# A decoder trunk on one core: six weight tiles of the output projection's second column block ahead of the tiles that meet the last heads

## The chip, the cores and the metric

The kernel runs on one core of one Trainium2 chip. The metric is the device time of one execution in microseconds (us), lower is better; the median of several runs is compared. The engines are TensorE (PE in the profile; its weight loads are PEld), VectorE (DVE), ScalarE (ACT), GpSimd (POOL) and SyncE (SP), which here issues DMA transfers. Each engine takes its own instructions in a fixed order.

## The reference

One decoder layer on 256 tokens of width 2048, all in float32. What matters here is the middle: the gated DeltaNet output of 16 heads of 128, gated, plus a gated pooling branch, goes through one output projection with a residual; its result is normalised and enters the MLP.

```python
o = rmsnorm(o, gdn_norm_w[l]) * jax.nn.silu(z.reshape(bsz, seq, N_HEADS, HEAD_DIM))
y_a = o.reshape(bsz, seq, D_LIN)
...
mixed = jax.nn.sigmoid(g_a) * y_a + jax.nn.sigmoid(g_b) * y_b
x = x + jnp.einsum('bsd,de->bse', mixed, w_out[l])

h = rmsnorm(x, norm_ffn_w[l])
gate, up = jnp.split(jnp.einsum('bsd,df->bsf', h, w_up[l]), 2, axis=-1)
```

`mixed` is 256 x 2048 and `w_out` is 2048 x 2048. The sum over d for one output column needs all 16 heads.

## The kernel before, in words

**Weights.** Every weight matrix is streamed once, as tiles of 256 rows by 512 columns (512 KB), in one list `srcs` (L79 to L95) that fixes the order of loading. For each tile `begin` (L105 to L120) starts a load into `raw` (four buffers) on SP's queue, a cast into `whi` on ScalarE (L112) and the rest `raw - whi` into `wlo` on VectorE (L119). `whi` and `wlo` have three buffers each. `weights()` hands out the next tile of the list and starts those up to two tiles further on (`AHEAD = 2`). A buffer is written again when the matmuls that read it are done.

**Matmuls.** `gemm_a` (L138 to L153) makes a 256 x 512 block of a product. A weight tile covers two steps k of 128 rows; for each, and each half t of the tokens, there are three matmuls of 128x128 by 128x512: high part of the activations times `whi` (L149), low part times `whi` (L150), high part times `wlo` (L151). So a weight tile is twelve matmuls, and a block of 2048 rows is eight tiles. The block accumulates in a PSUM tile of the pool `psm`, of which there are two (L62). With `steps` and `ps` a call does only some of the tiles and goes on with a PSUM tile begun before.

**Heads.** The heads are made in four groups g of four. The small matmuls and vector work of a group are dealt out by `side()` between the big matmuls of the input projection. When a group is through, `gated` (L779) forms its gated sum `sz` (L781, L782), and `mixed` (L791) transposes `sz` on PE (`turned`, eight transposes, L194) into PSUM; ScalarE copies that to `mhi` (L794) and VectorE takes the rest to `mlo` (L795). `mhi[g]`, `mlo[g]` are the activations of rows 512g to 512g + 511 of the output projection. Its weight tiles 6 and 7 of each block, and only those, meet group 3.

**The output projection.** Four column blocks of 512. Since group 3 is finished last, L805 begins the first blocks with the tiles that do not need it: tiles 0 to 5 of block 0 and 0, 1 of block 1, in the two PSUM tiles. Then come `gated` and `mixed` of group 3, the end of the pool `mix`, the load of x into `xt` on ScalarE's queue (L813), the rest of blocks 0 and 1, and blocks 2 and 3. After each block VectorE adds its PSUM tile to `xt` (L823), which frees it, ScalarE takes sums of squares (L826), PE transposes the block (L832), and ScalarE and VectorE scale it into `fhl` (L836, L837), the input of the MLP. The MLP's first matmuls are `gemm_b` (L173, L174).

**Order.** The kernel is written as one stream of instructions. Before it is built, a planner (the tile framework, with `schedule_with_timeline_sim=True`) fixes each engine's order from its own estimate of times; an instruction that is not ready by that estimate can stand behind one that comes later in the source. On the chip nothing is reordered.

Of the kernel before, what the change touches and what calls it, by code (L numbers as in the profile page):

```python
# [17 lines left out]
KD = D // P  # L18
# [15 lines left out]
def kernel(  # L34
# [32 lines left out]
    def nm(s):  # L67
        cnt[0] += 1
        return f"{s}_{cnt[0]}"

    def pg(shape=(P, 512)):
        return psg.tile(list(shape), F32, tag="g", name=nm("psg"))


    def cols(w, base, nk):
        return [w[c * 256 : (c + 1) * 256, base : base + 512].rearrange("(k p) f -> p k f", p=P)
                for c in range(nk // 2)]

    srcs = []  # L79
# [8 lines left out]
            srcs += cols(w_in[0], base + 512 * g, KD)  # L88
    outw = [cols(w_out[0], 512 * c, KD) for c in range(4)]

    srcs += outw[0][:6] + outw[1][:2] + outw[0][6:] + outw[1][2:] + outw[2] + outw[3]
    for c in range(DFF // 512):
        srcs += cols(w_up[0], 512 * c, KD) + cols(w_up[0], DFF + 512 * c, KD)
    down = [cols(w_down[0], 512 * c, KF) for c in range(4)]
# [4 lines left out]
    def weights():  # L99

        begin(taken[0] + AHEAD + 1)
        taken[0] += 1
        return made[taken[0] - 1]
# [21 lines left out]
    def side():  # L125
        next(side_work[0], None)
# [5 lines left out]
    def pm():  # L132
        return psm.tile([P, 2, 512], F32, tag="m", name=nm("psm"))
# [4 lines left out]
    def gemm_a(lh, ll, nk, steps=None, ps=None):  # L138

        ps = pm() if ps is None else ps  # L140
        for c in range(nk // 2) if steps is None else steps:
            if c == 1:
                while later:
                    later.pop(0)()
            hi, lo = weights()
            for kk in range(2):
                k = 2 * c + kk
                for t in range(2):
                    mm(ps[:, t, :], lh(k, t), hi[:, kk, :], start=(k == 0), stop=False)  # L149
                    mm(ps[:, t, :], ll(k, t), hi[:, kk, :], start=False, stop=False)  # L150
                    mm(ps[:, t, :], lh(k, t), lo[:, kk, :], start=False, stop=(k == nk - 1))  # L151
                side()
        return ps  # L153
# [3 lines left out]
    def gemm_b(rhl, nk):  # L157

        banks[0] ^= 1
        if banks[0]:
            pair = [pm(), pm()]
            ps = [pair[f // 2][:, f % 2].rearrange("p (a s) -> p a s", a=2) for f in range(4)]
        else:
            ps = [pg([P, 2, S]) for f in range(4)]
        for c in range(nk // 2):
            hi, lo = weights()
            for f in range(4):
                fs = slice(f * P, (f + 1) * P)  # L170
                for kk in range(2):
                    k = 2 * c + kk
                    mm(ps[f], hi[:, kk, fs], rhl(k), start=(k == 0), stop=False, skip_group_check=True)  # L173
                    mm(ps[f][:, 1, :], lo[:, kk, fs], rhl(k)[:, 0, :], start=False, stop=(k == nk - 1),  # L174
                       skip_group_check=True)
        return ps
# [242 lines left out]
    for g, win in enumerate(WINDOWS):  # L419
# [3 lines left out]
        for cs in (slice(0, P + PAD), slice(P + PAD, NB)):  # L423
            b = bd[:, cs]
            n = cs.stop - cs.start
# [15 lines left out]
    mhi = []  # L441
    mlo = []
# [277 lines left out]
    for g in range(4):  # L720
        kq = mp.tile([P, 4, 2, S], F32, tag="kq", bufs=1, name=nm("kq"))
        for kind, dst in ((1, kq[:, :, 0, :]), (0, kq[:, :, 1, :])):
            ps = ps_k0 if kind == 1 and g == 0 else gemm_a(xh, xl, KD)
# [15 lines left out]
        ps = gemm_a(xh, xl, KD)  # L739
# [26 lines left out]
        ps = gemm_a(lambda k, t: phi[:, k, t * P : (t + 1) * P], lambda k, t: plo[:, k, t * P : (t + 1) * P], 4)  # L766
# [4 lines left out]
        ps = gemm_a(xh, xl, KD)  # L771
# [7 lines left out]
        def gated(sz=sz, res=res, yb=yb):  # L779
            drain()  # L780
            nc.vector.tensor_tensor(sz, res[0].rearrange("p t h d -> p t (h d)"), sz, op=ALU.mult)  # L781
            nc.vector.tensor_tensor(sz, sz, yb, op=ALU.add)  # L782
# [17 lines left out]
    def at(tiles):  # L800
        return lambda k, t: tiles[k // 4][:, k % 4, t * P : (t + 1) * P]

    early = [gemm_a(at(mhi), at(mlo), KD, range(n)) for n in (6, 2)]  # L805
    gated()
    mixed()
    mix.__exit__(None, None, None)
# [7 lines left out]
    ssq4 = cpool.tile([P, 2, 4], F32, tag="ssq4", name="ssq4b")  # L816
    for c in range(4):
        if c < 2:
            ps = gemm_a(at(mhi), at(mlo), KD, range((6, 2)[c], 8), early[c])
        else:  # L820
            ps = gemm_a(at(mhi), at(mlo), KD)
        xs = xt[:, :, c * 512 : (c + 1) * 512]
        nc.vector.tensor_tensor(xs, xs, ps, op=ALU.add)  # L823
        for t in range(2):
            jk = cpool.tile([P, 512], F32, tag="sqj", name=nm("sqj"))
            nc.scalar.activation(jk, xs[:, t, :], AF.Square, accum_out=ssq4[:, t, c : c + 1])  # L826
        for k2 in range(2):
            pt = pg([P, 2, S])
            for kk in range(2):
                k = 4 * c + 2 * k2 + kk  # L830
                for t in range(2):
                    nc.tensor.transpose(pt[:, kk, t * P : (t + 1) * P], xt[:, t, k * P : (k + 1) * P], ident)  # L832
            for kk in range(2):
                k = 4 * c + 2 * k2 + kk
                nw = vec[:, V_FFN + k : V_FFN + k + 1]
                nc.scalar.activation(fhi[:, k, :], pt[:, kk, :], AF.Copy, scale=nw)  # L836
                nc.vector.scalar_tensor_tensor(flo[:, k, :], pt[:, kk, :], nw, fhi[:, k, :].bitcast(F32),  # L837
                                               op0=ALU.mult, op1=ALU.subtract)
# [9 lines left out]
    for c in range(DFF // 512):  # L848
        ps = gemm_b(lambda k: fhl[:, k], KD)
# [12 lines left out]
        ps = gemm_b(lambda k: fhl[:, k], KD)  # L862
# [15 lines left out]
    for c in range(2):  # L878
        ps = pm()
# [72 lines left out]
```

## Time and profile before

| | |
|---|---|
| median of 3 runs | 1586.81 us (1585.77 to 1587.41) |
| the profiled execution | 1584.99 us, its span 1582.9 us, mean granted clock 0.997 |
| bytes read from HBM | 297.56 MB, 191 GB/s over the span |
| w_out tiles | 32 loads of 512 KB, median 3.8 us to landing |
| casts L112, subtractions L119 | 530 of 1053 ns, 528 of 1224 ns |

A row of a timeline gives the start in us, the duration in us, the engine, the line, the operation, what it writes and reads, how many were merged (x), and in brackets how long the engine stood idle before it and what released it. A row of a table by windows gives the window, its length, and the busy time of each engine in it with the number of instructions (x), then the granted clock, the DMA engines' busy share and GB/s. Matmuls overlap one another in the records, so the pace is read from their starts.

### The profile page before, as it was taken

The numbers are of one execution on the slowest core, as the hardware profiler recorded it, in microseconds if no ns is written. First come the engines' busy times: TensorE is split into PE (matmuls) and PEld (weight loads), VectorE is DVE, ScalarE is ACT, GpSimd is POOL, SyncE is SP. The second block draws the span as 40 slices with busy tenths as digits, with TensorE's granted clock in tenths as the row PEclk, the third lists the DMA queues.
The fourth block names the chain that finished last, engine by engine and source line by source line (L and its number), as shares of the span: only waits on it lengthen the run. The fifth ranks groups of instructions, "written<-read, shape, count | busy, mean of one in ns | idle before, by whom it ended". The sixth has DMA issues, their size and how long they took to land.

```text
span 1582.9 us, 21262 instructions
## 1 busy us (share of the span) xinstructions
PE 1561.9 (99%) x8052; PEld 1311.6 (83%) x8052; DVE 1067.9 (67%) x1619; ACT 746.3 (47%) x953; POOL 44.5 (3%) x69
## 2 busy tenths in 40 slices
PE   8999999999999999999999999999999999999997
PEld 6888888888878888788788888888888888888885
DVE  6798758885698757795555666666766667444445
ACT  6554435444555445544454544444444444333334
POOL 3010000000000000000000000000000000000000
PEclk9999999999999999999999999999999999999998
DMA  8667657776667757675556666666666666666664
GB/s 277 184 208 208 192 147 204 212 211 174 180 207 201 201 147 200 208 206 170 197 182 181 190 192 187 187 188 189 184 197 188 187 188 213 198 193 193 195 192 131
DMA packets 167924, 304.22 MB, mean 192 GB/s; under 512 B 19186, under 2 KB 22274, under 8 KB 167694
## 3 DMA queue, kind: packets, MB, share of 16 engines
q1 hardware_dynamic: 165088, 298.36, 63.9%
q10 hardware_dynamic: 2734, 4.51, 0.9%
q8 instruction: 63, 1.03, 0.2%
q14 instruction: 39, 0.32, 0.1%
HBM read 297.56 MB, written 5.27 MB: 191 GB/s over the span
## 4 chain that ended last, share of the span: by engine, by line
PE 96%; DVE 1%; DMA 1%; issue 1%; ACT 0%; SPq 0%; DVEq 0%; POOLq 0%; POOL 0%
PE psm L151 15%; PE psm L150 15%; PE psm L149 15%; PE psm L173 10%; PE psg L173 10%; PE psg L174 5%; PE psm L174 5%; PE psg L886 3%; PE psg L887 3%; PE psg L888 3%; PE psm L886 2%; PE psm L887 2%; PE psm L888 2%; PE psg L561 1%; PE psg L194 1%
## 5 line engine op out<-in xcount | busy, mean ns | idle before, releaser
L119 DVE TENSOR_TENSOR wlo<-raw,whi 128x1024 fp32r<-128x1024 f32 x528 | 645.6, 1224 | 424.2 <-ACT whi L112 415.7
L112 ACT CAST whi<-raw 128x1024 fp32r<-128x1024 f32 x530 | 557.7, 1053 | 746.0 <-PE psm L150 325.1
L149 PE MATMUL psm<-whi,xhl 128*128 128x512 f32 x896 | 352.3, 393 | 1.9 <-ACT xhl L238 1.9
L151 PE MATMUL psm<-wlo,xhl 128*128 128x512 f32 x896 | 352.6, 394 | 0.9 <-DVE wlo L119 0.9
L150 PE MATMUL psm<-whi,xhl 128*128 128x512 f32 x896 | 351.8, 393 | 0.0
L173 PE MATMUL psm<-fhl,whi 128*128 128x512 f32 x704 | 245.9, 396 | 0.0
L173 PE MATMUL psg<-fhl,whi 128*128 128x512 f32 x704 | 237.8, 394 | 0.0
L149 PEld LDWEIGHTS psm<-whi,xhl 128*128 128x128 f32 x896 | 168.6, 188 | 36.5 <-ACT xhl L238 2.3
L151 PEld LDWEIGHTS psm<-wlo,xhl 128*128 128x128 f32 x896 | 168.6, 188 | 35.9 <-DVE wlo L119 1.8
L150 PEld LDWEIGHTS psm<-whi,xhl 128*128 128x128 f32 x896 | 168.6, 188 | 34.7
L174 PE MATMUL psm<-fhl,wlo 128*128 128x256 f32 x704 | 194.2, 279 | 0.0
L174 PE MATMUL psg<-fhl,wlo 128*128 128x256 f32 x704 | 178.6, 279 | 0.0
L173 PEld LDWEIGHTS psm<-fhl,whi 128*128 128x128 f32 x704 | 131.4, 188 | 30.3
L173 PEld LDWEIGHTS psg<-fhl,whi 128*128 128x128 f32 x704 | 129.2, 188 | 24.0
L174 PEld LDWEIGHTS psg<-fhl,wlo 128*128 128x128 f32 x704 | 132.5, 188 | 6.9
L174 PEld LDWEIGHTS psm<-fhl,wlo 128*128 128x128 f32 x704 | 132.5, 188 | 1.1
L886 PE MATMUL psg<-whi,hhi 128*128 128x512 f32 x176 | 68.6, 390 | 0.0
L886 PE MATMUL psm<-whi,hhi 128*128 128x512 f32 x176 | 68.5, 389 | 0.0
L887 PE MATMUL psm<-whi,hlo 128*128 128x512 f32 x176 | 68.5, 389 | 0.0
L887 PE MATMUL psg<-whi,hlo 128*128 128x512 f32 x176 | 68.5, 389 | 0.0
L888 PE MATMUL psm<-wlo,hhi 128*128 128x512 f32 x176 | 68.5, 389 | 0.0
L888 PE MATMUL psg<-wlo,hhi 128*128 128x512 f32 x176 | 61.7, 389 | 0.0
(234 smaller groups left out, 1438.7 us busy)
## 6 DMA issues: line engine op xcount, KB each, us to landing
raw<-in_w_in_dram SPq DMA_DIRECT2D x226, 512.0 KB, 4.2
raw<-in_w_up_dram SPq DMA_DIRECT2D x176, 512.0 KB, 4.0
raw<-in_w_down_dram SPq DMA_DIRECT2D x88, 512.0 KB, 4.3
raw<-in_w_out_dram SPq DMA_DIRECT2D x32, 512.0 KB, 3.8
mv<-vrow SPq DMA_DIRECT2D x12, 512.0 KB, 5.4
taps<-in_conv_qkv_w_dram SPq DMA_DIRECT2D x16, 256.0 KB, 5.7
raw<-in_pool_w_dram SPq DMA_DIRECT2D x8, 512.0 KB, 5.0
x<-in_x_dram SPq DMA_DIRECT2D x4, 512.0 KB, 7.2
```

Source lines behind the costliest of these rows:

```text
L112: nc.scalar.copy(hi, raw)
L119: nc.vector.tensor_tensor(lo, raw, hi.bitcast(F32), op=ALU.subtract)
L149: mm(ps[:, t, :], lh(k, t), hi[:, kk, :], start=(k == 0), stop=False)
L150: mm(ps[:, t, :], ll(k, t), hi[:, kk, :], start=False, stop=False)
L151: mm(ps[:, t, :], lh(k, t), lo[:, kk, :], start=False, stop=(k == nk - 1))
L173: mm(ps[f], hi[:, kk, fs], rhl(k), start=(k == 0), stop=False, skip_group_check=True)
L174: mm(ps[f][:, 1, :], lo[:, kk, fs], rhl(k)[:, 0, :], start=False, stop=(k == nk - 1), skip_group_check=True)
L194: nc.tensor.transpose(pt[:, ff, t * P : (t + 1) * P], src[:, t, f * P : (f + 1) * P], ident)
L561: mm(pg0, kq[:, h, 0, 0:P], kq[:, h, :, :], start=True, stop=True)
L886: mm(acc[c][t], lh(k, t), hi[:, kk, :], start=(k == 0), stop=False)
L887: mm(acc[c][t], ll(k, t), hi[:, kk, :], start=False, stop=False)
L888: mm(acc[c][t], lh(k, t), lo[:, kk, :], start=False, stop=(k == KF - 1))
```

## The change

Two places, which belong together: the order of loading, and how many tiles of block 1 are multiplied ahead of group 3's `gated` and `mixed`.

```diff
-    srcs += outw[0][:6] + outw[1][:2] + outw[0][6:] + outw[1][2:] + outw[2] + outw[3]
+    srcs += outw[0][:6] + outw[1][:6] + outw[0][6:] + outw[1][6:] + outw[2] + outw[3]
...
-    early = [gemm_a(at(mhi), at(mlo), KD, range(n)) for n in (6, 2)]
+    early = [gemm_a(at(mhi), at(mlo), KD, range(n)) for n in (6, 6)]
     gated()
     mixed()
...
         if c < 2:
-            ps = gemm_a(at(mhi), at(mlo), KD, range((6, 2)[c], 8), early[c])
+            ps = gemm_a(at(mhi), at(mlo), KD, range(6, 8), early[c])
```

Tiles 2 to 5 of block 1 move from behind tiles 6 and 7 of block 0 to ahead of them, in the list of loads and in the source's order of matmuls. Twelve tiles now come ahead of group 3's `gated` and `mixed` in the source, not eight, and two tiles of block 1 remain behind block 0's end, not six. Nothing else changes: the number of loads, casts, subtractions, matmuls and transposes, the buffers and the arithmetic of each block are the same.

## The prediction

> **What bounds the kernel now.** I began with the page: busy times, then the chain that ended last.
>
> ```profile
> span 1582.9 us, 21262 instructions
> PE 1561.9 (99%) x8052; PEld 1311.6 (83%) x8052; DVE 1067.9 (67%) x1619; ACT 746.3 (47%) x953; POOL 44.5 (3%) x69
> ...
> PE 96%; DVE 1%; DMA 1%; issue 1%; ACT 0%; SPq 0%; DVEq 0%; POOLq 0%; POOL 0%
> ```
>
> TensorE is the bound. The change neither adds nor removes a matmul, so only idle PE time can be won, or new idle time made. The second view, stretches of 20 us (busy time of PE, PEld, DVE, ACT, POOL; then granted clock), shows where PE idles inside the run:
>
> ```profile
> 640.00:660.00 20.00, 19.72 (x84) 15.33 (x83) 16.96 (x27) 8.53 (x12) 1.91 (x1) 1.00 0.74 229
> 660.00:680.00 20.00, 19.35 (x93) 15.99 (x92) 15.04 (x24) 10.70 (x17) 0.00 (x0) 1.00 0.66 204
> ...
> 760.00:780.00 20.00, 18.29 (x92) 14.30 (x92) 12.42 (x17) 5.81 (x8) 1.64 (x1) 1.00 0.46 155
> 780.00:800.00 20.00, 20.00 (x94) 16.64 (x93) 12.51 (x13) 11.72 (x20) 0.00 (x0) 1.00 0.70 237
> ```
>
> Of what touches the change, 760 to 780 alone is not full: 1.71 us idle. The third view is PE's timeline there (start, duration; in brackets the idle time and its releaser):
>
> ```profile
> 762.44 0.48 PE L149 MATMUL psm<-whi,mhi 128*128 128x512 f32 x1
> ...
> 767.77 0.39 PE L151 MATMUL psm<-wlo,mhi 128*128 128x512 f32 x1
> 769.07 0.50 PE L149 MATMUL psm<-whi,mhi 128*128 128x512 f32 x1 [0.91 <-ACT whi L112]
> 769.41 0.40 PE L150 MATMUL psm<-whi,mlo 128*128 128x512 f32 x1
> 770.33 0.50 PE L151 MATMUL psm<-wlo,mhi 128*128 128x512 f32 x1 [0.52 <-DVE wlo L119]
> ...
> 772.50 0.39 PE L151 MATMUL psm<-wlo,mhi 128*128 128x512 f32 x1
> 772.81 1.06 PE L194 MATMUL psg<-ident,sz 128*128 128x128 f32 x8
> 773.80 0.50 PE L149 MATMUL psm<-whi,mhi 128*128 128x512 f32 x1
> ...
> 774.37 0.41 PE L149 MATMUL psm<-whi,mhi 128*128 128x512 f32 x1
> 775.06 0.50 PE L151 MATMUL psm<-wlo,mhi 128*128 128x512 f32 x1 [0.28 <-DVE wlo L119]
> ...
> 782.71 0.39 PE L149 MATMUL psm<-whi,mhi 128*128 128x512 f32 x1
> ...
> 788.15 0.40 PE L149 MATMUL psm<-whi,mhi 128*128 128x512 f32 x1
> 788.39 1.04 PE L832 MATMUL psg<-ident,xt 128*128 128x128 f32 x8
> 789.18 0.48 PE L150 MATMUL psm<-whi,mlo 128*128 128x512 f32 x1
> 789.50 0.39 PE L151 MATMUL psm<-wlo,mhi 128*128 128x512 f32 x1
> ```
>
> To price the loss I count matmuls into the output projection's PSUM tiles. Each window's PE count also holds one that still ran at its left edge, except the first's:
>
> ```profile
> 762.40:772.70 10.30, 8.83 (x36) 6.53 (x36) 0.00 (x0) 0.00 (x0) 1.00 0.41 132
> 772.70:788.10 15.40, 14.21 (x61) 11.27 (x61) 1.22 (x1) 0.00 (x0) 1.00 0.81 280
> 782.65:788.10 5.45, 5.45 (x25) 4.51 (x25) 1.22 (x1) 0.00 (x0) 1.00 0.93 344
> ```
>
> The quiet pace: 24 matmuls from 782.71 to 788.15, 5.44 us, so 0.227 each and 2.72 per weight tile of twelve. From 762.44 to 788.15 there are 36 + 60 = 96; at that pace 21.76 us. Eight transposes cost, by the undisturbed L832 ones, 789.50 - 788.15 less two matmuls: 0.90. The first gap after other work is 0.09 too long. So 25.71 - 21.76 - 0.90 - 0.09 = **2.96 us** are lost here, more than the page's idle time, since a matmul's end is modelled. Gap by gap: 767.77 to 769.07 is 1.07 over the pace and the next gap 0.11; 769.41 to 770.33 0.69 and the next 0.10; 774.37 to 775.06 0.46 and the next 0.11. That is 2.54; 0.42 is spread.
>
> Why PE waits there is in ScalarE's and VectorE's timelines:
>
> ```profile
> 765.25 1.05 ACT L112 CAST whi<-raw 128x1024 fp32r<-128x1024 f32 x1 [1.93 <-PE psm L150]
> 767.97 1.04 ACT L112 CAST whi<-raw 128x1024 fp32r<-128x1024 f32 x1 [1.67 <-PE psm L150]
> 772.70 1.05 ACT L112 CAST whi<-raw 128x1024 fp32r<-128x1024 f32 x1 [3.68 <-DVE sz L782]
> 773.65 0.58 ACT L794 CAST mhi<-psg 128x512 fp32r<-128x512 f32 x1
> 773.98 0.39 ACTq L813 DMA_DIRECT2D xt<-in_x_dram  x1
> ```
>
> ```profile
> 766.34 1.23 DVE L119 TENSOR_TENSOR wlo<-raw,whi 128x1024 fp32r<-128x1024 f32 x1
> ...
> 769.05 1.23 DVE L119 TENSOR_TENSOR wlo<-raw,whi 128x1024 fp32r<-128x1024 f32 x1 [0.28 <-ACT whi L112]
> 770.19 1.22 DVE L781 TENSOR_TENSOR sz<-on,sz 128x1024 f32<-128x1024 f32 x1
> 771.44 1.22 DVE L782 TENSOR_TENSOR sz<-sz,yb 128x1024 f32<-128x1024 f32 x1
> 773.78 1.23 DVE L119 TENSOR_TENSOR wlo<-raw,whi 128x1024 fp32r<-128x1024 f32 x1 [1.11 <-ACT whi L112]
> 774.92 1.28 DVE L795 TENSOR_TENSOR mlo<-psg,mhi 128x512 fp32r<-128x512 f32 x2
> ...
> 782.91 1.22 DVE L823 TENSOR_TENSOR xt<-xt,psm 128x1024 f32<-128x1024 f32 x1 [0.64 <-PE psm L151]
> ```
>
> Write (b, i) for weight tile i of column block b. From 762.44 PE takes (1,0) and (1,1). The next tiles loaded are (0,6) and (0,7), which need the last heads. They sit in two of the three whi/wlo buffers, one of them cast at 765.25 and left unused. So (1,2), which the planner lets PE take ahead of them, is cast only at 767.97, into the buffer that (1,1) has just left, and PE stands for it. Likewise (1,3), cast at 772.70 when (1,2) ends. (The row names L782, but it ended in the same instant, 771.44 + 1.22.) PE thus already runs (1,2) ahead of the transposes today, but with one buffer turning instead of three.
>
> **The change, part by part.** (a) Loading (1,2) to (1,5) ahead of (0,6), (0,7). SP issues the same 512 KB loads, four of them earlier by two places: no cost. The cast of 765.25 and the one before it now serve (1,3) and (1,2). So (1,2) starts at 767.77 + 0.23 = 768.00, and (1,3), its wlo done at 766.34 + 1.23, follows at once. That removes the 2.54 itemised. Of the 0.42 spread I take a little: **-2.6 us**, at most -2.96. If this cover were gone the loss would be the old one.
>
> (b) Where the eight transposes of sz go. They are ready at 771.44 + 1.22 = 772.66. PE's order is fixed ahead, and the trace shows it made by readiness: the matmul at 774.37, the first of (0,6), stands inside (1,3), behind the two that needed only whi and ahead of those that waited for wlo. In the new kernel PE works without a pause on (1,2) to 770.72; then that buffer is free, (1,5) is cast from 770.7 to 771.75, and its wlo must wait on VectorE for L782, begun at 771.44, so it ends near 773.9. The transposes are ready between: they go behind two matmuls of (1,5) and ahead of its other ten. They cost 0.90 as before.
>
> (c) The handshake after them. From the transposes' start to the first half of mlo: 774.92 + 0.64 - 772.81 = 2.75 us, of which PE itself works 0.90. Nothing but (1,5) can cover it, since (0,6), (0,7) and (1,6) all need the new heads. Ten matmuls are 2.27 us, more than the 1.85 needed: cost 0. With the transposes behind all of (1,5), the cover is gone: 1.85, less the one or two matmuls that need mhi alone, about 1.6. So the new cost has the bounds 0 and 1.85, and I take 0, by the 0.3 us between L782's start and the end of the cast. What would be late next is the first L150 of (0,6).
>
> (d) The load of x for L823 is issued on ScalarE's queue behind the transposes (773.98, 1.17 after their start). Two tiles of block 0 follow the transposes and ten matmuls: 34 x 0.227 + 0.90 = 8.6 us to L823, where it was 10.1. Issue to landing:
>
> ```profile
> xt<-in_x_dram ACTq DMA_DIRECT2D x4, 512.0 KB, 4.8
> ```
>
> 1.17 + 4.8 = 6.0 us, so 2.6 us are spare: cost 0.
>
> (e) Block 1 now ends two tiles after block 0, not four: 5.44 us. Block 2 needs block 0's PSUM pair, which L823 frees 1.26 us after block 0's end: hidden. ScalarE has each block's squares and scalings close together:
>
> ```profile
> L836 ACT ACTIVATE fhl<-psg,vec 128x256 fp32r<-128x256 f32 x16 | 7.0, 473 | 3.7 <-DVE fhl L837 2.8 <-PE psg L832 0.8
> L826 ACT ACTIVATE sqj<-xt 128x512 f32<-128x512 f32 x8 | 5.1, 633 | 1.8 <-DVE xt L823 1.7
> ```
>
> 4 x 0.47 + 2 x 0.63 = 3.2 us a block, in pieces under 2 us. A cast begins two tiles ahead, 5.44 us, and with its subtraction takes 1.05 + 1.23, so it may be 3.2 us late: cost 0; a whole block's work in front of one cast would just use that up.
>
> Sum: -2.6 us. On the profiled execution, 1584.99 us (span 1582.9 and 2.1 around it), that gives 1582.4. The median of the runs, 1586.81, lies 1.82 above it; so **1584.2 us**.
>
> **The rivals.** *Handshake exposed.* L782 and the cast of (1,5) are 0.3 us apart; a plan that puts wlo first delays sz by 1.23, and the transposes fall behind (1,5). Then -2.6 + 1.6 = -1.0: 1585.8. For it: in the trace the cast and wlo of 772.70 and 773.78 did go ahead of L794 and L795.
>
> *Everything in reach is won.* The plan is made anew, and besides the 2.96 the 0.28 + 0.65 idle between 640 and 680 go: 1582.9. Against: that stage comes before the moved tiles.
>
> *The change doesn't bite.* PE already ran (1,2) early; should the planner leave PE in today's order, 1586.8. Against: who holds the buffers does change.
>
> *Slower: x comes late to L823.* ScalarE takes its queue in order. If the plan sets L813 behind the cast that waits for block 1's end, then with block 0's end at 788.15 - 2.6 = 785.55 and block 2 due at 791.0, the cast ends at 792.0, x lands at 796.8, and L823 frees the pair at 798.1: 7.1 us of standing, net +4.5: 1591.3. One cast earlier it is 2.72 less, 1588.6. It decides from an issue after 791.0 - 1.22 - 4.8 = 785.0. Against: L813 now follows the transposes by 1.17 us.
>
> *Slower clock.* If nothing at all covers (c) and PE runs at half clock for as long as it stood: 1.85 + 1.5 - 2.6, so 1587.5. Here the largest pause, 1.3 us between starts, left the granted clock at 1.00. The Trainium skill ("TensorE: Matmul & The Clock Gate", the section on why this matters) warns of idle gaps above about 3 us; by that rule the gap of (c) would be too short and the time stays as forecast.
>
> **How the numbers follow.** A measurement of this kernel tells 0.2%, 3.17 us, from no change. The three runs lie from 1585.77 to 1587.41, so a median may be off by 0.8. Forecast 0.43 (0.16 of it reads faster, being 0.6 short of the bound; its own range is 1583.3 to 1585.2); everything won 0.08 (0.07 faster); exposed 0.21; no bite 0.06; x late 0.18 (0.14 slower); clock 0.04. Faster 0.23, slower 0.14, same 0.63. The range, 1582.8 to 1588.8, leaves out most of the late x and the tail below.
>
> **What would show it.** (a) No wait for whi or wlo at L149 and L151 in the six tiles before the transposes of sz, and the casts one tile apart. (b) Those transposes inside (1,5). (c) No PE gap at the first L150 of (0,6); a gap of 1.6 there means the exposed case. (d) L813 within some 1.2 us of the transposes, and no wait of L823 for a DMA. (e) No PE wait at the start of block 2. The prediction is wrong if PE still idles more than 1 us in this stage, or if a new wait shows in blocks 2 and 3.

## The result and the profile after

The changed kernel takes 1583.2 us (median of 15 runs, 1580.49 to 1585.09) against 1585.94 us for the kernel before beside it (15 runs, 1582.99 to 1587.41): ratio 0.9983, interval 0.9976 to 0.9990. That is 2.7 us less; the forecast was 2.6 us less. The forecast of the time itself, 1584.2, lies 1.0 us above the median, nearly all of it because the kernel before came out at 1585.94 here and not at 1586.81. The interval stands for 1.6 to 3.8 us less, so that 2.7 agrees with 2.6 to a tenth is luck; the test of the sum is the stage, below.

The page of the changed kernel, the same three lines as before:

```profile
span 1580.7 us, 21261 instructions
...
PE 1560.8 (99%) x8052; PEld 1312.2 (83%) x8052; DVE 1067.6 (68%) x1619; ACT 745.9 (47%) x953; POOL 44.4 (3%) x69
...
PE 97%; DMA 1%; DVE 1%; issue 1%; ACT 0%; SPq 0%; DVEq 0%; POOLq 0%; POOL 0%
```

The same matmuls, the same bound. The table by windows of the changed kernel:

```profile
640.00:660.00 20.00, 20.00 (x86) 15.88 (x86) 17.65 (x27) 8.66 (x10) 1.91 (x1) 1.00 0.78 241
660.00:680.00 20.00, 19.44 (x94) 16.08 (x93) 15.00 (x24) 11.27 (x18) 0.00 (x0) 1.00 0.68 212
...
760.00:780.00 20.00, 20.00 (x107) 17.15 (x107) 13.68 (x18) 7.16 (x9) 1.64 (x1) 1.00 0.44 139
```

PE's 18.29 us of 760 to 780 are now 20.00: the stage has no hole left. Its PE timeline:

```profile
771.42 0.39 PE L149 MATMUL psm<-whi,mhi 128*128 128x512 f32 x1
...
774.14 0.39 PE L149 MATMUL psm<-whi,mhi 128*128 128x512 f32 x1
...
776.86 0.39 PE L149 MATMUL psm<-whi,mhi 128*128 128x512 f32 x1
777.08 0.39 PE L150 MATMUL psm<-whi,mlo 128*128 128x512 f32 x1
777.32 1.03 PE L194 MATMUL psg<-ident,sz 128*128 128x128 f32 x8
778.11 0.48 PE L151 MATMUL psm<-wlo,mhi 128*128 128x512 f32 x1
...
780.48 0.39 PE L149 MATMUL psm<-whi,mhi 128*128 128x512 f32 x1
780.71 0.39 PE L150 MATMUL psm<-whi,mlo 128*128 128x512 f32 x1
```

The first three rows are the starts of (1,3), (1,4) and (1,5), 2.72 us apart, the quiet pace, with no bracket. The transposes of group 3 stand behind two matmuls of (1,5); ten more follow, and (0,6) begins at 780.48 and goes on to its first L150 without a pause. ScalarE and VectorE, in that order, in the changed kernel:

```profile
768.67 1.05 ACT L112 CAST whi<-raw 128x1024 fp32r<-128x1024 f32 x1 [1.67 <-PE psm L150]
771.39 1.06 ACT L112 CAST whi<-raw 128x1024 fp32r<-128x1024 f32 x1 [1.67 <-PE psm L150]
774.11 1.06 ACT L112 CAST whi<-raw 128x1024 fp32r<-128x1024 f32 x1 [1.66 <-PE psm L150]
...
778.45 2.91 ACTq L813 DMA_DIRECT2D xt<-in_x_dram  x4
...
791.48 1.05 ACT L112 CAST whi<-raw 128x1024 fp32r<-128x1024 f32 x1 [1.69 <-DMA raw<-in_w_out_dram]
```

```profile
772.15 1.22 DVE L782 TENSOR_TENSOR sz<-sz,yb 128x1024 f32<-128x1024 f32 x1
773.30 1.22 DVE L119 TENSOR_TENSOR wlo<-raw,whi 128x1024 fp32r<-128x1024 f32 x1
...
786.12 1.22 DVE L823 TENSOR_TENSOR xt<-xt,psm 128x1024 f32<-128x1024 f32 x1 [0.63 <-PE psm L151]
```

The casts are one tile apart. That of (1,5), begun at 771.39, ends at 772.45; L782 had begun at 772.15, so wlo of (1,5) went behind it, at 773.30.

The span fell by 2.2 us and not by the stage's gain, so the **stage** is measured by itself from here on: from the first matmul of the output projection to the last group of L832 transposes. Kernel before, then changed kernel:

```profile
737.70 0.39 PE L149 MATMUL psm<-whi,mhi 128*128 128x512 f32 x1
...
842.86 1.04 PE L832 MATMUL psg<-ident,xt 128*128 128x128 f32 x8
```

```profile
738.40 0.39 PE L149 MATMUL psm<-whi,mhi 128*128 128x512 f32 x1
...
840.61 1.04 PE L832 MATMUL psg<-ident,xt 128*128 128x128 f32 x8
```

105.16 us before, 102.21 after: **2.95 us**, all that the prediction's ledger (2.96) had found to be lost. The stage begins 0.7 us later in this execution; in the runs below, whose work up to there is the same, it begins anywhere from 735.95 to 739.25, so one pair of profiles can't put that 0.7 down to the change. The three with the old list of loads begin at 735.95 to 737.70, the eight with a new list at 737.24 to 739.25; whether the lean to later is chance stays open. PE takes the same instructions in the same order up to there in both kernels, as far as the traces record them.

### The profile page after: what moved, and what is told of

Read it like the earlier page. It is cut to its first block, busy times and chain, and to the rows that moved or that the text cites. A ratio compares the mean times of both kernels' runs of the same rounds, so it can differ in the third digit from the quotient of the medians.

```text
span 1580.7 us, 21261 instructions
## 1 busy us (share of the span) xinstructions
PE 1560.8 (99%) x8052; PEld 1312.2 (83%) x8052; DVE 1067.6 (68%) x1619; ACT 745.9 (47%) x953; POOL 44.4 (3%) x69
## 4 chain that ended last, share of the span: by engine, by line
PE 97%; DMA 1%; DVE 1%; issue 1%; ACT 0%; SPq 0%; DVEq 0%; POOLq 0%; POOL 0%
PE psm L151 15%; PE psm L150 15%; PE psm L149 15%; PE psm L173 10%; PE psg L173 10%; PE psg L174 5%; PE psm L174 5%; PE psg L886 3%; PE psg L887 3%; PE psg L888 3%; PE psm L886 2%; PE psm L887 2%; PE psm L888 2%; PE psg L561 1%; PE psg L194 1%
## 5 line engine op out<-in xcount | busy, mean ns | idle before, releaser
L150 PE MATMUL psm<-whi,xhl 128*128 128x512 f32 x896 | 351.8, 393 | 0.0
L150 PEld LDWEIGHTS psm<-whi,xhl 128*128 128x128 f32 x896 | 168.7, 188 | 34.6
```

## The experiments

The theory: two of three whi/wlo buffers were held by (0,6) and (0,7), which nothing could use yet, and PE stood for the casts in the one that still turned. The rival: what helps is more matmuls ahead of the late heads in the source, which hide the wait for `sz` and for the transposes. The stage is read in each profile as above; ratios are to the kernel before on the same chip. A ratio's interval is some 1.4 us either way, about the size of the steps tested here, so the conclusions rest on the stage. It is read from one profile a run; the changed kernel twice and e1 gave 102.21, 102.22 and 102.22, the kernel before and e2 105.16 both.

| run | first matmul | last L832 | stage | ratio, interval |
|---|---|---|---|---|
| e1_only_loads | 738.61 | 840.83 | 102.22 | 0.9979, 0.9970 to 0.9988 |
| e2_only_order | 737.19 | 842.35 | 105.16 | 0.9995, 0.9986 to 1.0004 |
| e3_late_sz | 737.70 | 841.64 | 103.94 | 0.9987, 0.9978 to 0.9996 |
| e4_late_sz_before | 735.95 | 841.35 | 105.40 | 1.0000, 0.9992 to 1.0009 |
| e5_three_ahead | 738.72 | 842.92 | 104.20 | 0.9997, 0.9988 to 1.0005 |
| e6_four_ahead | 739.25 | 842.38 | 103.13 | 0.9990, 0.9981 to 0.9999 |
| e7_five_ahead | 737.24 | 840.37 | 103.13 | 0.9989, 0.9980 to 0.9998 |
| e8_again | 738.14 | 840.36 | 102.22 | 0.9986, 0.9978 to 0.9995 |
| e9_x_late | 737.55 | 846.59 | 109.04 | 1.0023, 1.0013 to 1.0033 |

**The two halves of the change, each alone.** To part them, `weights` takes the tile's place in the list (`place`), so that the source's order of matmuls and the order of loading can differ. First the loads alone:

```diff
-    srcs += outw[0][:6] + outw[1][:2] + outw[0][6:] + outw[1][2:] + outw[2] + outw[3]
+    outat = len(srcs)
+    srcs += outw[0][:6] + outw[1][:6] + outw[0][6:] + outw[1][6:] + outw[2] + outw[3]
...
+    place = ((0, 1, 2, 3, 4, 5, 12, 13), (6, 7, 8, 9, 10, 11, 14, 15))
+    early = [gemm_a(at(mhi), at(mlo), KD, range(n), tiles=place[c]) for c, n in enumerate((6, 2))]
```

> Only the list of loads is changed, (1,2) to (1,5) ahead of (0,6), (0,7); the matmuls keep the old order in the source. Theory (two of three whi/wlo buffers were held by tiles that could not be used): the loads alone give it all, the stage from the first matmul of the output projection to the last group of L832 transposes takes 102.2 us as in the changed kernel (105.2 before), ratio 0.998 to the kernel before. Rival (what helps is that more matmuls stand ahead of the late heads in the source, which hides the wait for sz and the transposes): nothing without the second edit, stage 105.2, ratio 1.000.

Measured 102.22 us and ratio 0.9979: the list of loads alone gives the whole gain. Then the matmuls alone:

```diff
+    outat = len(srcs)
     srcs += outw[0][:6] + outw[1][:2] + outw[0][6:] + outw[1][2:] + outw[2] + outw[3]
...
+    place = ((0, 1, 2, 3, 4, 5, 8, 9), (6, 7, 10, 11, 12, 13, 14, 15))
+    early = [gemm_a(at(mhi), at(mlo), KD, range(n), tiles=place[c]) for c, n in enumerate((6, 6))]
```

> Only the order of the matmuls in the source is changed, six tiles of block 1 ahead of the late heads; the loads keep the old list. Theory: (0,6) and (0,7) still hold two buffers, so PE waits as before at (1,2) and (1,3): stage 105.2 us, ratio 1.000. Rival: most of the gain, stage 102.2 to 103, ratio 0.998.

Measured 105.16 us, the old stage to the hundredth, with the old three waits on PE (here the lines have moved by two):

```profile
768.56 0.50 PE L151 MATMUL psm<-whi,mhi 128*128 128x512 f32 x1 [0.91 <-ACT whi L114]
...
769.82 0.50 PE L153 MATMUL psm<-wlo,mhi 128*128 128x512 f32 x1 [0.52 <-DVE wlo L121]
...
774.55 0.50 PE L153 MATMUL psm<-wlo,mhi 128*128 128x512 f32 x1 [0.28 <-DVE wlo L121]
```

The rival is out: the order in the source is worth nothing by itself. The planner moved the matmuls of block 1 ahead by itself, with and without the second edit; what it could not do was give them buffers. Two things were not tried: more `whi` and `wlo` buffers with the old list, which would test the buffers without any other order, and a plan with PE's order held fixed (with the new list PE takes four tiles of block 1 ahead of block 0's end and not two).

**The handshake, exposed.** One more VectorE operation that leaves `sz` as it is makes it 1.2 us later:

```diff
             nc.vector.tensor_tensor(sz, sz, yb, op=ALU.add)
+            if g == 3:
+                for _ in range(1):
+                    nc.vector.tensor_tensor(sz, sz, sz, op=ALU.max)
```

> The changed kernel with one more VectorE operation of 1.22 us (maximum of sz with itself) between L782 and the transposes of group 3. Theory: sz is ready 1.2 us later, after wlo of (1,5), so the transposes fall behind all of (1,5) and the handshake transposes, mhi, mlo has nothing over it: PE waits about 1.6 us (bounds 0.5 and 1.85) at the first L150 of (0,6), stage 103.8 us against 102.2. Rival: the handshake is hidden anyway, stage 102.2 to 102.4.

Measured 103.94, so 1.72 us more than 102.22. PE in this run (lines behind the edit have moved by three: L797 is L794, L798 is L795):

```profile
778.88 1.03 PE L194 MATMUL psg<-ident,sz 128*128 128x128 f32 x8
780.43 0.73 PE L149 MATMUL psm<-whi,mhi 128*128 128x512 f32 x2 [0.52 <-ACT mhi L797]
781.81 0.50 PE L150 MATMUL psm<-whi,mlo 128*128 128x512 f32 x1 [0.64 <-DVE mlo L798]
```

The transposes now stand behind the last matmul of (1,5), and PE waits first for `mhi`, then for `mlo`: the prediction's rival "handshake exposed", with its price of 1.6. The same operation in the kernel before:

> The kernel before with the same extra operation. Theory: PE waits for the casts of (1,2) and (1,3) and not for sz, so 1.2 us more on sz changes little: stage 105.2 us, within 0.4 either way. Rival (PE's loss before was the wait for sz): stage 106.4 us, the operation's whole 1.2 us on top.

105.40, 0.24 more. In that run PE waits for casts, as it did, and the transposes run without a wait of their own:

```profile
767.32 0.50 PE L149 MATMUL psm<-whi,mhi 128*128 128x512 f32 x1 [0.91 <-ACT whi L112]
768.58 0.50 PE L151 MATMUL psm<-wlo,mhi 128*128 128x512 f32 x1 [0.53 <-DVE wlo L119]
...
772.05 0.50 PE L149 MATMUL psm<-whi,mhi 128*128 128x512 f32 x1 [0.91 <-ACT whi L112]
...
772.62 1.03 PE L194 MATMUL psg<-ident,sz 128*128 128x128 f32 x8
```

So before the change `sz` was not what PE waited for.

**How many tiles ahead.** The change with 3, 4 and 5 for the second 6, in the list and in `early`:

```diff
+    srcs += outw[0][:6] + outw[1][:3] + outw[0][6:] + outw[1][3:] + outw[2] + outw[3]
...
+    early = [gemm_a(at(mhi), at(mlo), KD, range(n)) for n in (6, 3)]
```

> Three tiles of block 1 ahead, not two and not six. Theory (held buffers): (1,2) is freed of its wait, (1,3) is still cast only when (1,2) ends: loses 1.0 to 1.9 us of the 2.96, stage 103.2 to 104.1 us (105.2 before, 102.2 with six). Rival (cover for the late heads: each tile ahead hides 2.7 us): one tile more than before is enough, stage 102.2 to 102.5.

104.20, a tenth above the theory's range: besides the wait for the cast of (1,3), the transposes came before `sz` was there. Three tiles ahead:

```profile
772.81 0.50 PE L149 MATMUL psm<-whi,mhi 128*128 128x512 f32 x1 [0.91 <-ACT whi L112]
773.15 0.40 PE L150 MATMUL psm<-whi,mlo 128*128 128x512 f32 x1
773.85 1.06 PE L194 MATMUL psg<-ident,sz 128*128 128x128 f32 x8 [0.30 <-DVE sz L782]
```

> Four tiles of block 1 ahead. Theory: (1,4) is the tile that turns in one buffer, but the transposes of sz stand in its wait for the cast; only the wait for its wlo stays, about 0.6 to 0.9 us: stage 102.8 to 103.1 us. Rival: all hidden, 102.2.

> Five tiles of block 1 ahead. Theory: as with four, (1,5) is cast when (1,4) ends and the transposes of sz stand in that wait: 0.6 to 0.9 us lost at its wlo, stage 102.8 to 103.1 us. Rival: all hidden, 102.2.

Both 103.13, 0.03 above the theory's range. Four tiles ahead:

```profile
774.99 1.03 PE L194 MATMUL psg<-ident,sz 128*128 128x128 f32 x8
776.06 0.50 PE L149 MATMUL psm<-whi,mhi 128*128 128x512 f32 x1
...
777.32 0.50 PE L151 MATMUL psm<-wlo,mhi 128*128 128x512 f32 x1 [0.28 <-DVE wlo L119]
```

The wait for the last tile's cast is filled by the transposes; the wait for its `wlo` stays. With five it is the same wait, 0.28 us at 778.03. Each step moves the one tile that has a single buffer one further, until with six there is none.

**The changed kernel again.**

> The changed kernel again, beside the others on one chip. Stage 102.2 us, ratio 0.998. How far the time ahead of the stage (738.4 us in the changed kernel's profile, 737.7 before) moves from one execution to the next shows here: theory, it is the same plan and moves by up to 1 us of itself; rival, the change costs 0.7 us there each time.

102.22. Its windows ahead of the stage, the same work as in both kernels:

```profile
640.00:660.00 20.00, 19.92 (x84) 15.51 (x83) 17.16 (x27) 8.16 (x11) 1.91 (x1) 1.00 0.74 235
660.00:680.00 20.00, 19.38 (x93) 16.03 (x93) 14.79 (x24) 11.06 (x17) 0.00 (x0) 1.00 0.67 208
```

0.08 + 0.62 us idle here, 0.56 in the other profile of the same kernel: this stage moves by itself.

**x late.** The prediction's slower rival, put on the chip: the first quarter of x's load is made to wait for block 0's end. (The rival had all four quarters late. Here the other three are issued as before and stand ahead of the first on ScalarE's queue.)

```diff
-    for c in range(4):
+    for c in range(1, 4):
         cs = slice(c * 512, (c + 1) * 512)
         nc.scalar.dma_start(xt[:, :, cs], x[0, :, cs].rearrange("(t p) d -> p t d", p=P))
...
         xs = xt[:, :, c * 512 : (c + 1) * 512]
+        if c == 0:
+            nc.scalar.copy(xt[:, 0, 0:1], ps[:, 0, 0:1])
+            nc.scalar.dma_start(xs, x[0, :, 0:512].rearrange("(t p) d -> p t d", p=P))
```

> The changed kernel with the first quarter of x's load held back: one element of xt is first written by ScalarE from block 0's PSUM tile, and the load of that quarter is issued behind it, so not before block 0 ends (about 786.1 us in the changed kernel's profile). It puts the prediction's slower rival on the chip: a load of x issued after 785.0 keeps L823 from freeing block 0's PSUM pair in time for block 2. Theory: issue near 786.5, landing after 4.8 to 8.4 us (medians of the two profiles), L823 1.22 us, so block 2 begins 1.5 to 5 us late, stage 103.7 to 107 us against 102.2. Rival (something else hides it): stage 102.2 to 102.5.

109.04, 6.8 us more, above the range. ScalarE's issue and VectorE's sum in this run (L826 is L823, moved by three, and L835 is L832):

```profile
786.18 0.37 ACTq L825 DMA_DIRECT2D xt<-in_x_dram  x1
```

```profile
793.55 2.35 DVE L826 TENSOR_TENSOR xt<-xt,psm 128x1024 f32<-128x1024 f32 x2 [3.47 <-DMA xt<-in_x_dram]
```

7.4 us from issue to L826. And PE, then its windows (the figure behind POOL's is the granted clock):

```profile
790.29 0.39 PE L151 MATMUL psm<-wlo,mhi 128*128 128x512 f32 x1
794.98 1.94 PE L835 MATMUL psg<-ident,xt 128*128 128x128 f32 x8 [4.30 <-DMA raw<-in_w_out_dram]
796.57 0.78 PE L149 MATMUL psm<-whi,mhi 128*128 128x512 f32 x1
...
797.57 0.63 PE L151 MATMUL psm<-wlo,mhi 128*128 128x512 f32 x1
797.99 0.63 PE L149 MATMUL psm<-whi,mhi 128*128 128x512 f32 x1
```

```profile
792.50:793.00 0.50, 0.00 (x0) 0.00 (x0) 0.00 (x0) 0.00 (x0) 0.00 (x0) 1.00 0.90 348
793.00:793.50 0.50, 0.00 (x0) 0.00 (x0) 0.00 (x0) 0.00 (x0) 0.00 (x0) 0.52 0.61 234
...
794.00:796.00 2.00, 1.02 (x5) 1.05 (x6) 2.00 (x3) 0.72 (x2) 0.00 (x0) 0.50 0.22 84
...
798.00:800.00 2.00, 2.00 (x6) 1.57 (x5) 0.76 (x3) 1.60 (x6) 0.00 (x0) 0.54 0.74 244
800.00:802.00 2.00, 2.00 (x10) 1.64 (x9) 0.20 (x2) 1.05 (x1) 0.00 (x0) 1.00 0.05 18
```

PE stood 4.30 us, by the row's bracket (the releaser named there is doubtful: VectorE had just finished the sum that the transposes read). The clock fell to 0.50 within the pause, at 793.0, and when work came back matmuls start 0.42 apart instead of 0.227 until near 800. Of the 6.8 us, 794.98 - 790.29 less one matmul, 4.5, is the wait itself; the other 2.3 is put down to the slow clock, and some 4.8 us at half speed (794.98 to 799.8) would lose about that, 2.4. The expectation had the wait and missed the clock.

## Why the prediction was right, point by point

**(a) The buffers: right, the term a little small.** The three waits are gone. Of the 2.96 us in reach the sum took 2.6, because I gave away most of the 0.42 us that I could not pin to a gap; the stage got 2.95. Those small widenings went with the waits, and a difference over the whole stretch was the better price than the sum of the gaps. That only the loads matter, and not the source's order of matmuls, the prediction half saw (PE "already runs (1,2) ahead") but kept both edits in one term; e1 and e2 part them.

**(b) The place of the transposes: right to the matmul.** Behind two of (1,5), ahead of ten. On the chip `sz` was ready at 772.15 + 1.22 = 773.37 and the transposes began at 777.32, so their place comes from PE's order, fixed by the planner, and not from when `sz` was ready there. e3 agrees with the reasoning by readiness: with `sz` 1.2 us later, behind wlo of (1,5), they fall behind the tile. The margin of 0.3 us between L782's start and the end of the cast was 772.45 - 772.15 = 0.30; that it decides is not shown, for no run moved it by as little, and the planner's own times were not looked at.

**(c) The handshake: right.** Cost 0 with ten matmuls over it; 1.72 us in e3 without them, where 1.6 was said, within the bounds of 0 and 1.85.

**(d) The load of x: right in effect, priced from the wrong load.** L813 followed the transposes by 1.13 us and L823 waited for PE alone. But the row of 4.8 us holds the one landing of the four that the trace of before has, that of the second quarter, issued at 774.39. The row of the changed kernel:

```profile
xt<-in_x_dram ACTq DMA_DIRECT2D x4, 512.0 KB, 8.5
```

It holds two: 8.4 for the second quarter, 8.7 for the third, counted in the order of issue. The first quarter, the only one that block 0's L823 reads, has no landing in either trace. In the changed kernel it was there within 786.12 - 778.45 = 7.7 us of its issue; in e3 its landing is on record:

```profile
xt<-in_x_dram ACTq DMA_DIRECT2D x1, 512.0 KB, 6.4
```

With 6.4 the load would have landed at 784.85, so an estimate of the spare time is 1.3 us, half of the prediction's 2.6, and the rival's point of no return was nearer to 791.0 - 1.22 - 6.4 = 783.4 than to the prediction's 785.0. (The 7.4 us of e9's first quarter were spent behind the other three.) Had it come to that, the rival's price was too low as well, since it left out the clock.

**(e) Blocks 0 and 1 close together: right.** PE goes from block 1 through the transposes into block 2 without a wait: last matmul at 791.14, transposes from 791.37, first matmul of block 2 at 792.16. One cast, at 791.48, waited 1.7 us for its weights to land, inside the slack of 3.2 us.

**The rivals.** Exposed handshake: real, not taken. Everything won: the idle time at 640 to 680 is no part of it; it moves between profiles of one kernel. No bite: out by the stage, 2.95 us shorter. x late: a real mechanism, shown by e9, and not touched by this change. Slower clock: as the prediction put it, with nothing over (c), it did not come, for e3 left (c) open and the granted clock stayed at 1.00; a longer pause, e9's, did bring it. The rival's 1.5 us for the clock does not follow from its own words (half speed over 1.85 us loses 0.9); e9's 2.3 came after a pause of 4.30. No run points to a version that beats the changed kernel in this stage: it has no PE wait left.

## What to carry to other kernels

When a planner or a queue lets work run ahead of tiles that cannot be used yet, look at who holds the buffers: a tile that is loaded early and used late takes a buffer out of the turn, and the work that overtakes it runs on what is left. Load in the order in which the tiles can be used, and move the late ones behind everything that can go before. Price such a loss over the whole stretch against the quiet pace, not by the visible gaps alone.

## What the runs showed of the hardware

A PE pause of 4.30 us (e9) halved the granted clock. The last matmul before it ended at 790.68; the clock was 1.00 up to 793.0 and 0.50 from there on, 2.3 us into the pause. It stayed at half for 5 us after work came back (794.98 to 800), with 3.4 us of matmuls among them: about 2.3 us on top of the pause. Idle times of 0.52 and 0.64 us (e3) left it at 1.00:

```profile
778.00:782.00 4.00, 2.84 (x16) 1.96 (x15) 2.51 (x4) 2.02 (x3) 0.00 (x0) 1.00 0.67 216
```

The Trainium skill ("TensorE: Matmul & The Clock Gate", the section on why this matters) puts the limit at idle gaps of about 3 us; both runs agree with it. That the clock in e9 was down 2.3 us into the pause leaves open whether a pause shorter than 3 us could already cost it.

A load of 512 KB of x on ScalarE's queue took 4.8 us (second quarter, before), 6.4 (first quarter, e3), 8.4 (second quarter, changed kernel) and 8.7 (third), beside the same weight stream shifted by a few us. Why was not tried.
